# Copying a row to all partitions: products with constant matrices replaced by DMAs through DRAM, in a two-layer decoder trunk

## The chip, the cores and the metric

The kernel runs on one core of a Trainium2 chip. The metric is the device time of one execution in microseconds. A core has five engines that run their own instruction streams in order: TensorE (PE, matrix products into PSUM; its weight loads are listed as PEld), VectorE (DVE), ScalarE (ACT), GpSimd (POOL) and SyncE (SP), which here only issues DMAs. Streams wait for each other by semaphores, and for DMAs in the same way. DMAs are issued from SP, ACT or POOL and carried by 16 DMA engines.

## What is computed

Two layers over 512 tokens of width 1024. Each layer normalises x, multiplies it with one wide matrix, runs sliding-window attention and an mLSTM on slices of the result, merges both under gates, and adds a squared-ReLU MLP. Cut to what the change touches:

```python
def rmsnorm(x, gain):
    x32 = x.astype(jnp.float32)
    inv = lax.rsqrt(jnp.mean(x32 * x32, axis=-1, keepdims=True) + EPS)   # one factor per token
    return (x32 * inv).astype(x.dtype) * gain

h = rmsnorm(x, norm_mix)
z = h @ w_in
q_a, k_a, v_a, q_m, k_m, v_m, o_m, if_m, gates = jnp.split(z, splits, axis=-1)
...
# mLSTM, per head and chunk: a running maximum over the tokens keeps the exponentials bounded
log_d = jnp.where(causal, b[..., :, None] - b[..., None, :] + log_i[..., None, :], -jnp.inf)
m_t = jnp.maximum(log_inter, jnp.max(log_d, axis=-1))
w = jnp.exp(log_d - m_t[..., None]) * jnp.einsum('bnhlk,bnhsk->bnhls', q, k)
...
g_a, g_m = jnp.split(gates, 2, axis=-1)
mixed = jax.nn.sigmoid(g_a) * (att @ w_att_branch) + jax.nn.sigmoid(g_m) * (hm @ w_m_branch)
x = x + mixed @ w_out
x = x + relu(rmsnorm(x) @ W1)^2 @ W2
```

## The kernel before

Tokens go in four blocks of 128 (`NB`), features in eight (`KT`). Every weight matrix is streamed from DRAM in chunks of 128 x 512 (SP issues the loads), and each chunk is split into a high part `wh` (ACT, L165) and a low part `wl` (DVE, L166), both in a reduced-precision float32 form; the activations are split in the same way. One block of a product is then three matmuls (`mm3`): high x high, high x low, low x high. A chunk feeds four blocks, which go to four PSUM banks; a group is eight chunks (four for the branch projections), and after it ACT or DVE empties the four banks (`evac`). There are five banks for these products and three, `aux`, for everything else. The split tiles have four buffers.

The mixer of a layer (`mixer`) runs the groups in this order: q, then k, v and the gate logits (264 columns), then the mLSTM's q and k (`ev_qk`), two groups of branch gates, the mLSTM's v (`ev_v`, banks emptied by ACT at L711), the two halves of the attention projection, and more. Into these, `weave` puts the side work at given places: attention by units of a block and a kv head (`att_scores`, `att_softmax`, `att_probs`, `att_out`), the mLSTM's gating (`gating0` to `gating3`), and for each of its four heads `m_decay`, `m_weights` and `m_out`. A scheduler then settles the order of each engine's stream from the dependencies, priorities and its own costs; the order on ACT, DVE and POOL follows from that.

Two places copy a row to all 128 partitions.

**The norm's factor.** It exists as a column, one value per token and partition (`norm.col`, 128 x 4, last written at L244). q and k/v of the attention, and v of the mLSTM, have tokens on the partitions and use the column. The mLSTM's q and k and the branch gates have tokens along the free dimension and need the factor as a row of 512 in every partition. `along` makes it: four DVE multiplies build diagonal matrices from the identity (L297), a product with a matrix of ones sums them in PSUM, and ACT copies the result to SBUF (L302). The row is read by DVE in `ev_qk` (L665, L667) and for the gates (L699). Behind it on POOL come the squares of q (L505), whose sums DVE takes (L506).

**The running maxima.** `gating2` makes `cm`, four rows (one per head) of 512 running maxima, by scans on DVE (L474). `gating3` splits them into a high part on partitions 0 to 3 and a low part on partitions 32 to 35 of `cm2` (L492, L493). `m_decay` multiplies `cm2` with a selector `sel`, prepared by POOL for each layer, so that one head's row appears in all partitions of an `aux` bank, and ACT copies it to a temporary (L741). `m_weights` reads it: DVE takes a maximum (L748), ACT exponentials (L749, L752), POOL masks the triangle (L754), and DVE multiplies with a product of keys and queries (L760).

Of the kernel before, what the change touches and what calls it, by code (L numbers as in the profile page):

```python
# [8 lines left out]
F32 = mybir.dt.float32  # L9
F32R = mybir.dt.float32r  # L10
BF16 = mybir.dt.bfloat16
I32 = mybir.dt.int32
AF = mybir.ActivationFunctionType
ALU = mybir.AluOpType
AX = mybir.AxisListType

P = 128
T = 512
NB = T // P
# [6 lines left out]
MH, MQK, MV = 4, 64, 128  # L26
# [7 lines left out]
def hybrid_kernel(ctx, tc, x, norm_mix, w_in, att_q_norm, att_k_norm, att_sinks, m_gate_bias,  # L34
# [3 lines left out]
    ve, sc, gp = nc.vector, nc.scalar, nc.gpsimd  # L38

    latest = [None]  # L40
# [15 lines left out]
    small = ctx.enter_context(tc.tile_pool(name="small", bufs=3))  # L56

    inp = ctx.enter_context(tc.tile_pool(name="inp", bufs=2))

    uid = [0]  # L60

    def nm(s):
        uid[0] += 1
        return f"{s}_{uid[0]}"
# [4 lines left out]
    def pool(phase, name, bufs):  # L69
        now[name] = phase.enter_context(tc.tile_pool(name=name, bufs=bufs, reuse_waits="tile"))  # L70
        return now[name]
# [4 lines left out]
    def temp(dt=F32):  # L76
        return now["tmp"].tile([P, T], dt, tag="t", name=nm("t"))
# [14 lines left out]
    def aux(shape=(P, T)):  # L92
        return now["paux"].tile(list(shape), F32, tag="aux", name=nm("aux"))
# [4 lines left out]
    def f32(ap):  # L98
        return ap.bitcast(F32)


    start = ExitStack()
    psum_pools(start, 3)
    sc.preload_act_table_set(LN_EXP)
    ident = const.tile([P, P], F32, name="ident")
    make_identity(nc, ident)
    ones = const.tile([P, P], F32, name="ones")
# [5 lines left out]
                     pattern=[[1, P]], channel_multiplier=-1)  # L113
    gp.affine_select(out=tri_l, in_=ones, compare_op=ALU.is_ge, fill=0.0, base=0,
                     pattern=[[-1, P]], channel_multiplier=1)
# [130 lines left out]
    class Norm:  # L246
# [45 lines left out]
        def along(self):  # L292

            with tc.high_priority():
                dg = temp()
                for b in range(NB):
                    ve.tensor_scalar(dg[:, b * P:(b + 1) * P], ident, self.col[:, b:b + 1], None, op0=ALU.mult)  # L297
                pb = aux()
                with tc.issue_after(latest[0].ins):
                    pe.matmul(pb, ones, dg, start=True, stop=True)  # L300
                row = temp()
                sc.activation(row, pb, AF.Copy)  # L302
            return row


# [82 lines left out]
    def mixer(l, norm, late, order, phase):  # L388
# [6 lines left out]
        mid = pool(phase, "mid", 1)  # L395
# [8 lines left out]
        row = []  # L404
# [73 lines left out]
                                     gr[:, b:b + 1], op=ALU.add)  # L478


        sel = mid.tile([P, MH, P], F32R, tag="sel", name=nm("sel"))
        gp.memset(f32(sel), 0.0)
        for r in (0, 32):
            gp.affine_select(out=sel[r:r + MH], in_=ones[r:r + MH, 0:1].unsqueeze(2).to_broadcast([MH, MH, P]),
                             compare_op=ALU.is_equal, fill=0.0, base=0,
                             pattern=[[-1, MH], [0, P]], channel_multiplier=1)
        cm2 = mid.tile([P, T], F32R, tag="cm2", name=nm("cm2"))
        gp.memset(f32(cm2), 0.0)

        def gating3():  # L490
            cm = cms[0]
            sc.activation(cm2[0:MH, :], cm, AF.Copy)  # L492
            ve.tensor_tensor(cm2[32:32 + MH, :], cm, f32(cm2[0:MH, :]), op=ALU.subtract)  # L493
            cps = aux([P, NB * MH])
            for b in range(NB):
                pe.transpose(cps[:, b * MH:(b + 1) * MH], cm[:, b * P:(b + 1) * P], ident[:MH, :MH])
            ve.tensor_tensor(em.rearrange("p b h -> p (b h)"), cps,
                             bl[:, 0].rearrange("p b h -> p (b h)"), op=ALU.add)
            sc.activation(em, em, AF.Exp, scale=-1.0)
# [3 lines left out]
        for b in range(NB):  # L503
# [5 lines left out]
                         op=ALU.mult)  # L509
# [207 lines left out]
        for i, (b, kv) in enumerate(units):  # L717
# [6 lines left out]
            if kv == 0 and b + 1 < NB:  # L724
                if b + 2 < NB:
                    side += [(at + 1, lambda b=b: k_vec(b + 2)), (at + 1, lambda b=b: q_vec(b + 2))]
                side += [(at + 2 * 1.65 - 1.75, lambda b=b: k_tr(b + 1)), (at + 2 * 1.65 - 2.15, lambda b=b: q_tr(b + 1))]
        side += [(8.45 + 3.0 * i, f) for i, f in enumerate((gating0, gating1, gating2, gating3))]
        side += [(9.6 + 1.65 * n, lambda n=n: qk_split(n // 2, n % 2)) for n in range(8)]
        g0, s0 = gate_steps(0)  # L730
# [4 lines left out]
        cmbs, wts = {}, {}  # L735

        def m_decay(h):
            pb = aux()
            pe.matmul(pb, sel[:, h, :], cm2, start=True, stop=True)
            cmbs[h] = temp()  # L740
            sc.activation(cmbs[h], pb, AF.Copy)  # L741

        def m_weights(h, s):
            cmb = cmbs[h]
# [56 lines left out]
        for h in range(MH):  # L801
            at = 28 + 4.65 * h
            side.append((at, lambda h=h: m_decay(h)))
            for i in range(NB):
                side += [(at + 1.75 + 4.65 * i / NB, lambda h=h, i=i: m_weights(h, i)),
                         (at + 4.65 + -0.55 + 4.65 * (i + 0.5) / NB, lambda h=h, i=i: m_out(h, i))]
# [513 lines left out]
    for l in range(DEPTH):  # L1320
        with start if l == 0 else ExitStack() as phase:
            if l > 0:
                psum_pools(phase, 3)
            norm = mixer(l, norm, late, order, phase)
        late = norm.steps(1, 1.5, 0.5)
        with ExitStack() as phase:
            psum_pools(phase, 2)
            norm = mlp(l, norm, late, phase)
        late = norm.steps(0, 1.5, 0.5, lambda k, norm=norm: turn_behind(norm, k)) if norm else []
        order = [4, 5, 6, 7, 0, 1, 2, 3]  # L1330
# [40 lines left out]
```

## Time and profile before

| | us |
|---|---|
| median of 3 runs | 1303.78 |
| lowest and highest run | 1303.59, 1304.21 |
| span of the profiled execution | 1302.9 |
| ACT busy | 763.7 |
| DVE busy | 955.5 |
| POOL busy | 200.4 |
| first and last copy of the norm's row to SBUF (L302) starts at | 39.8, 684.4 |
| first and last copy of a head's maxima to SBUF (L741) starts at | 152.3, 844.1 |

The span runs from the first to the last instruction of one profiled execution; the time of a run lies a little above it, as it has what comes before and after. In the rows of the trace a line of the timeline gives the start in us, the duration in us, the engine, the source line, the operation, the tile that it writes and those that it reads, the shape, how many equal instructions are merged (x), and in brackets how long the engine had been idle and what released it. Matmul durations overlap, since matmuls are pipelined; the distance between their starts is what one costs. A row of the waits gives the waiting engine and operation, what it waited for, the total in us, the number of waits and the longest. A row of DMA issues gives what is loaded, the issuing queue, the count, the size and the median time in us from issue to landing.

### The profile page before, as it was taken

The numbers are of one execution on the slowest core, as the hardware profiler recorded it, in microseconds if no ns is written. First come the engines' busy times: TensorE is split into PE (matmuls) and PEld (weight loads), VectorE is DVE, ScalarE is ACT, GpSimd is POOL, SyncE is SP. The second block draws the span as 40 slices with busy tenths as digits, with TensorE's granted clock in tenths as the row PEclk, the third lists the DMA queues.
The fourth block names the chain that finished last, engine by engine and source line by source line (L and its number), as shares of the span: only waits on it lengthen the run. The fifth ranks groups of instructions, "written<-read, shape, count | busy, mean of one in ns | idle before, by whom it ended". The sixth has DMA issues, their size and how long they took to land. (4 is left out here: it accounts for less than half of the span.)

```text
span 1302.9 us, 19074 instructions
## 1 busy us (share of the span) xinstructions
PE 1291.5 (99%) x6978; PEld 1105.2 (85%) x6978; DVE 955.5 (73%) x1505; ACT 763.7 (59%) x1329; POOL 200.4 (15%) x281
## 2 busy tenths in 40 slices
PE   9999999999999999999999999999999999999998
PEld 6877788888889999999888778888888899999987
DVE  4699754475677897968948996545737878879797
ACT  5578755544466665656555787554445556665563
POOL 4511100000003021131115111000000030311210
PEclk9999999999999999999999999999999999999999
DMA  5422222372369888898124222223714597988953
GB/s 154 110 72 59 74 81 74 90 249 82 98 155 172 236 185 207 195 211 216 33 75 114 65 66 75 79 75 92 256 57 129 141 215 195 201 212 196 213 148 98
DMA packets 130542, 177.61 MB, mean 136 GB/s; under 512 B 9864, under 2 KB 78320, under 8 KB 130448
## 3 DMA queue, kind: packets, MB, share of 16 engines
q1 hardware_dynamic: 94208, 131.82, 32.7%
q0 software_dynamic: 35520, 44.17, 21.2%
q8 instruction: 55, 0.90, 0.3%
q10 hardware_dynamic: 720, 0.40, 0.1%
q14 instruction: 39, 0.32, 0.1%
HBM read 174.27 MB, written 2.10 MB: 135 GB/s over the span
## 5 line engine op out<-in xcount | busy, mean ns | idle before, releaser
L47 PE MATMUL mm<-i,wh 128*128 128x512 f32 (+1 forms) x1280 | 352.7, 362 | 0.0
L867 ACT ACTIVATE wh<-raw 128x1024 fp32r<-128x1024 f32 x212 | 223.1, 1056 | 181.1 <-PE mm L47 114.0
L868 DVE TENSOR_TENSOR wl<-raw,wh 128x1024 fp32r<-128x1024 f32 x212 | 255.2, 1218 | 74.2 <-ACT wh L867 72.3
L47 PEld LDWEIGHTS mm<-i,wh 128*128 128x128 f32 x1280 | 224.3, 189 | 32.1 <-DVE a L699 0.8
L166 DVE TENSOR_TENSOR wl<-w,wh 128x512 fp32r<-128x512 f32 (+1 forms) x208 | 140.8, 679 | 137.7 <-ACT wh L165 129.4
L47 PE MATMUL mm<-i,wl 128*128 128x512 f32 (+1 forms) x640 | 229.8, 360 | 0.0
L165 ACT ACTIVATE wh<-w 128x512 fp32r<-128x512 f32 (+1 forms) x208 | 127.0, 611 | 146.7 <-PE mm L47 122.8
L47 PE MATMUL mm<-wh,uh 128*128 128x512 f32 x440 | 171.8, 390 | 0.0
L47 PE MATMUL mm<-wl,uh 128*128 128x512 f32 x440 | 171.7, 390 | 0.0
L47 PE MATMUL mm<-wh,ul 128*128 128x512 f32 x440 | 171.2, 389 | 0.0
L1027 POOL DMA_DIRECT2D raw<-in_w_ff_dram x48 | 62.3, 1304 | 591.3 <-DMA raw<-in_w_ff_dram 316.9
L47 PE MATMUL mm<-wh,i 128*128 128x512 f32 (+1 forms) x512 | 150.6, 370 | 1.2 <-ACT wh L165 0.6
L47 PEld LDWEIGHTS mm<-i,wl 128*128 128x128 f32 x640 | 120.8, 189 | 18.1 <-DVE wl L868 0.4
L47 PEld LDWEIGHTS mm<-wh,i 128*128 128x128 f32 x512 | 92.0, 188 | 19.0 <-DVE i L179 2.1
L913 DVE SCALAR_TENSOR_TENSOR x<-mm,ms,x 128x512 f32<-128x512 f32 x126 | 90.4, 743 | 9.9 <-PE mm L47 9.9
L47 PEld LDWEIGHTS mm<-wh,ul 128*128 128x128 f32 x440 | 82.6, 188 | 17.4
L47 PEld LDWEIGHTS mm<-wh,uh 128*128 128x128 f32 x440 | 82.8, 188 | 16.1
L47 PEld LDWEIGHTS mm<-wl,uh 128*128 128x128 f32 x440 | 82.8, 188 | 15.6
L47 PE MATMUL mm<-wl,i 128*128 128x512 f32 (+1 forms) x256 | 93.0, 363 | 0.0
L47 PE MATMUL mm<-wh,a 128*128 128x512 f32 x256 | 81.3, 392 | 0.0
L47 PE MATMUL mm<-a,wh 128*128 128x512 f32 x256 | 80.5, 397 | 0.0
L47 PE MATMUL aux<-i,wh 128*128 128x256 f32 x384 | 69.5, 283 | 0.0
(259 smaller groups left out, 2161.0 us busy)
## 6 DMA issues: line engine op xcount, KB each, us to landing
raw<-in_w_ff_dram SPq DMA_DIRECT2D x144, 512.0 KB, 5.2
raw<-in_w_ff_dram POOLq DMA_DIRECT2D x84, 512.0 KB, 7.8
w<-in_w_in_dram SPq DMA_DIRECT2D x128, 256.0 KB, 2.6
w<-in_w_out_dram SPq DMA_DIRECT2D x32, 256.0 KB, 2.7
w<-in_w_att_branch_dram SPq DMA_DIRECT2D x16, 256.0 KB, 2.6
w<-in_w_m_branch_dram SPq DMA_DIRECT2D x16, 256.0 KB, 2.7
w<-in_w_in_dram SPq DMA_DIRECT2D x16, 128.0 KB, 2.1
out_dram<-x SPq DMA_DIRECT2D x7, 256.0 KB, 2.0
```

The source lines that it names most:

```text
L47: latest[0] = nc.tensor.matmul(*args, **kw)
L165: sc.activation(wh[:, :off], raw[:, :off], AF.Copy)
L166: ve.tensor_tensor(wl[:, :off], raw[:, :off], f32(wh[:, :off]), op=ALU.subtract)
L867: sc.activation(hi, src, AF.Copy)
L868: ve.tensor_tensor(lo, src, f32(hi), op=ALU.subtract)
L913: ve.scalar_tensor_tensor(xh[:, cc], ps[i][:, cc], ms[j][:, b:b + 1], xh[:, cc], op0=ALU.mult, op1=ALU.add)
L1027: gp.dma_start(to[h], src(h, i, j), accum_op=ALU.add)
```

## The change

Both copies go through DRAM. A pool of DRAM tiles, `rows`, is added. `along` writes the column to a DRAM line of 512 floats, token order, and reads that line back into all partitions of a temporary; both DMAs are issued from POOL. `gating3` writes the four rows of `cm` to a DRAM tile `decay`, and `m_decay` reads one head's row into all partitions of a temporary, again from POOL. The diagonal multiplies, the products with `ones` and `sel`, the copies from PSUM, `sel`, `cm2` and the split of `cm` fall away. What reads the rows is unchanged.

```diff
     inp = ctx.enter_context(tc.tile_pool(name="inp", bufs=2))
+    rows = ctx.enter_context(tc.tile_pool(name="rows", bufs=2, space=bass.MemoryType.DRAM))
...
         def along(self):
 
             with tc.high_priority():
-                dg = temp()
-                for b in range(NB):
-                    ve.tensor_scalar(dg[:, b * P:(b + 1) * P], ident, self.col[:, b:b + 1], None, op0=ALU.mult)
-                pb = aux()
-                with tc.issue_after(latest[0].ins):
-                    pe.matmul(pb, ones, dg, start=True, stop=True)
+                line = rows.tile([T], F32, tag="line", name=nm("line"))
+                gp.dma_start(line.rearrange("(b p) -> p b", p=P), self.col)
                 row = temp()
-                sc.activation(row, pb, AF.Copy)
+                gp.dma_start(row, line.partition_broadcast(P))
             return row
...
-        sel = mid.tile([P, MH, P], F32R, tag="sel", name=nm("sel"))
-        gp.memset(f32(sel), 0.0)
-        for r in (0, 32):
-            gp.affine_select(out=sel[r:r + MH], in_=ones[r:r + MH, 0:1].unsqueeze(2).to_broadcast([MH, MH, P]),
-                             compare_op=ALU.is_equal, fill=0.0, base=0,
-                             pattern=[[-1, MH], [0, P]], channel_multiplier=1)
-        cm2 = mid.tile([P, T], F32R, tag="cm2", name=nm("cm2"))
-        gp.memset(f32(cm2), 0.0)
+        decay = rows.tile([MH, T], F32, tag="decay", name=nm("decay"))
 
         def gating3():
             cm = cms[0]
-            sc.activation(cm2[0:MH, :], cm, AF.Copy)
-            ve.tensor_tensor(cm2[32:32 + MH, :], cm, f32(cm2[0:MH, :]), op=ALU.subtract)
+            gp.dma_start(decay, cm)
...
         def m_decay(h):
-            pb = aux()
-            pe.matmul(pb, sel[:, h, :], cm2, start=True, stop=True)
             cmbs[h] = temp()
-            sc.activation(cmbs[h], pb, AF.Copy)
+            gp.dma_start(cmbs[h], decay[h].partition_broadcast(P))
```

In the order of the changed streams, the four broadcasts of a layer stand on POOL behind the last attention mask (heads 0 and 1), behind the first mask of head 1 (head 2) and behind the first mask of head 2 (head 3); the exponentials and maxima of heads 1 to 3 stand earlier on ACT and DVE than before, ahead of or among the evictions of the mLSTM's v. The reductions of L506 stand among the weight splits of the k/v group, the first behind that of its fourth chunk. On PE, apart from the removed products, a few transposes and products of the attention stand some matmuls earlier.

## Prediction

> **What bounds the kernel now.** I read first the page's head, busy times and slices, then TensorE's waits.
>
> ```profile
> span 1302.9 us, 19074 instructions
> PE 1291.5 (99%) x6978; PEld 1105.2 (85%) x6978; DVE 955.5 (73%) x1505; ACT 763.7 (59%) x1329; POOL 200.4 (15%) x281
> PE   9999999999999999999999999999999999999998
> PEclk9999999999999999999999999999999999999999
> ```
> ```profile
> PE aux L47 <- ACT t L581: 2.0, 2, 1.3
> PE aux L47 <- POOL ones L108: 1.2, 1, 1.2
> PE aux L52 <- ACT wh L165: 1.1, 2, 0.6
> ```
>
> PE is busy for 99% of the span, in every slice and at the full granted clock; its three largest waits are 2.0, 1.2 and 1.1 us. So a matmul taken from PE's stream shortens the span by its own time, and a new wait lengthens it only where PE itself stops. ACT, DVE and POOL may wait as long as PE's next operand is ready.
>
> **What is removed from PE.** Per layer one fp32 product with `ones` and four with `sel`. Busy times overlap with neighbours, so the price is read from the starts around them; the last row has the count of the `sel` products.
>
> ```profile
> 38.60 0.28 PE L47 MATMUL mm<-wh,i 128*128 128x264 f32 x1
> 38.73 1.02 PE L47 MATMUL aux<-t,ones 128*128 128x512 f32 x2
> ...
> 39.83 0.40 PE L47 MATMUL mm<-wh,i 128*128 128x264 f32 x2
> ...
> 40.19 0.40 PE L47 MATMUL mm<-wh,i 128*128 128x264 f32 x2
> ```
> ```profile
> 151.03 0.40 PE L47 MATMUL aux<-cm,sel 128*128 128x512 f32 x1
> 151.27 0.40 PE L47 MATMUL mm<-wh,i 128*128 128x512 f32 x1
> ```
> ```profile
> L47 PE MATMUL aux<-cm,sel 128*128 128x512 f32 x8 | 3.2, 394 | 0.0
> ```
>
> A usual block of three matmuls lasts 40.19 - 39.83 = 0.36 us; the block with the `ones` product lasts 39.83 - 38.60 = 1.23. The product costs 0.87 us, twice 1.74. A `sel` product costs 151.27 - 151.03 = 0.24, eight cost 1.9. **PE loses 3.6 us.** The four L297 multiplies, both evictions (L302, L741), the split of `cm` (L492, L493) and POOL's fills and selects for `sel` and `cm2` go too; none released PE, so they count nothing.
>
> **What a copy through DRAM takes.** The trace has no such copy. The nearest rows:
>
> ```profile
> w<-in_w_att_branch_dram SPq DMA_DIRECT2D x16, 256.0 KB, 2.6
> w<-in_w_in_dram SPq DMA_DIRECT2D x16, 4.0 KB, 1.9
> gc<-in_att_q_norm_dram POOLq DMA_DIRECT2D x2, 0.4 KB, 2.5
> grow<-in_m_head_norm_dram POOLq DMA_DIRECT2D x1, 4.0 KB, 2.2
> grow<-in_norm_ffn_dram POOLq DMA_DIRECT2D x1, 8.0 KB, 3.8
> gbias<-in_m_gate_bias_dram POOLq DMA_DIRECT2D x1, 8.0 KB, 4.2
> cosx<-in_rope_cos_dram POOLq DMA_DIRECT2D x1, 32.0 KB, 6.6
> ```
>
> A broadcast writes 128 rows of 2 KB, 256 KB, like a weight chunk. From SP the size costs 2.6 - 1.9 = 0.7 us; a small quiet POOL issue lands after 2.2. I take L = 2.2 + 0.7 = 2.9 us from issue to landing. The low end is 2.2, as if size cost nothing; the high end is 6.6, the slowest POOL row, which ran beside the first loads of x. That 128 readers share one row seems cheap: `gbias`, read that way, took 4.2 against 3.8 for `grow`, unshared, in the same crowd; 4.2 + 0.7 = 4.9 is the middle case.
>
> A weighing of its own: the profile's row for POOL's issues in the busy MLP is
>
> ```profile
> L1027 POOL DMA_DIRECT2D raw<-in_w_ff_dram x48: 1280/1286/1469, 346.8 to 1218.7; - x48
> ```
>
> so no issue was held more than 0.18 us over the median. The Trainium skill ("SBUF — State Buffer", section "SBUF: two separate sides") speaks against the change: descriptors for a POOL-issued DMA cannot be written while VectorE holds the shared port, and such a DMA of some 620 ns took 3100 there. By that rule L grows by about 2.5 us (an estimate from the page) to the second rival's case; by the row it stays, and the row decides here.
>
> **The norm's factor (`along`).** POOL issues a write of 512 single elements to DRAM, waits until it has landed, then issues the broadcast. Both stand in POOL's queue ahead of the squares of q (L505), and POOL waits for them.
>
> ```profile
> 31.85 0.16 DVE L244 TENSOR_TENSOR ncol<-ncol,nru 128x4 f32<-128x4 f32 x1
> 33.41 4.43 POOL L505 TENSOR_TENSOR t<-a 128x512 f32<-128x512 f32 x4 [9.36 <-ACT a L407]
> 39.73 1.86 DVE L506 TENSOR_REDUCE ssq<-t 128x8 f32<-128x512 f32 x3
> 39.38 0.43 DVE L166 TENSOR_TENSOR wl<-w,wh 128x264 fp32r<-128x264 f32 x1 [1.00 <-ACT wh L165]
> 68.41 1.27 DVE L665 SCALAR_TENSOR_TENSOR a<-mm,t 128x512 f32<-128x512 f32 x2
> 671.15 0.16 DVE L244 TENSOR_TENSOR ncol<-ncol,nru 128x4 f32<-128x4 f32 x1
> 678.04 4.43 POOL L505 TENSOR_TENSOR t<-a 128x512 f32<-128x512 f32 x4 [29.14 <-ACT a L407]
> 8.48 0.94 POOL L353 DMA_DIRECT2D cosx<-in_rope_cos_dram  x1
> 12.13 0.55 POOL L361 DMA_DIRECT2D gbias<-in_m_gate_bias_dram  x1
> ```
>
> The factor is ready at 32.0. The single elements cost about 0.4 us more to issue than `gc` (0.94 for `cosx`' 512 pieces against 0.55 for 128), so the write lands near 32.0 + 2.5 + 0.4 = 34.9, and POOL is free at 35.5 after 0.55 for the second issue. The row itself is there near 38; its first reader, L665, starts at 68.4, so that latency is hidden 30 us deep.
>
> The danger is POOL's delay. In the changed order of layer 0 DVE's reductions L506 stand ahead of some weight splits: before the split for the sixth k/v chunk DVE has done three. A square lasts 1.11 us, a reduction and a split end 0.67 + 0.43 after the third, so that split ends 4.4 us after POOL is free. PE wants it at the sixth chunk: the fourth started at 38.7 (the `ones` product stands at its head), a chunk is four blocks, 1.44 us, and without the product the sixth starts at 41.6. POOL must be free by some 37.3. With 35.5 nothing stops; with `cosx`' 6.6 POOL is free at 39.2 and PE stops 1.9. In layer 1 the squares start 6.7 us after the factor (678.0 against 671.3), so even that end costs next to nothing. Term: 0, bounds 0 to 1.9.
>
> **The running maxima.** `decay` (8 KB) is written once the last scan (L474) is done, at 113.2 us, 6.7 us before POOL's next select at 119.9. The four broadcasts stand in POOL's queue: heads 0 and 1 behind the last attention mask, head 2 behind head 1's first mask, head 3 behind head 2's first. Since no product of PE orders them any longer, the exponentials of all four heads move forward on ACT, and ACT must finish them before it empties PE's banks of v.
>
> ```profile
> 112.68 0.47 DVE L474 TENSOR_TENSOR_SCAN t<-aux,mp,neg 4x128 f32<-4x128 f32 x1
> 119.89 0.64 POOL L634 TENSOR_SCALAR_AFFINE_SELECT t<-t 128x512 fp32r<-128x512 f32 x1 [13.43 <-DVE kT L561]
> 147.91 2.11 POOL L634 TENSOR_SCALAR_AFFINE_SELECT t<-t 128x512 fp32r<-128x512 f32 x3 [0.23 <-DVE t L176]
> 154.76 0.39 ACT L749 ACTIVATE t<-t,bias 128x128 f32<-128x128 f32 x1
> 155.06 0.39 ACT L752 ACTIVATE t<-t,bias 128x128 f32<-128x128 f32 x1
> 161.16 2.05 ACT L711 ACTIVATE vm<-mm,ncol 128x512 f32<-128x512 f32 x3 [0.41 <-PE mm L47]
> 163.92 0.63 PE L47 MATMUL mm<-a,wh 128*128 128x512 f32 x2
> 806.41 2.05 ACT L711 ACTIVATE vm<-mm,ncol 128x512 f32<-128x512 f32 x3 [0.41 <-PE mm L47]
> ```
>
> On the old clock: the selects end at 150.0, so head 0 lands at 150.0 + L. Eleven exponentials at 0.30 and a weight split (0.53) follow until head 1's first mask may run: 3.8, the mask 0.3, then head 2's copy: it lands at 154.1 + 2L. Behind it on ACT stand one exponential (0.3, with DVE's maximum 0.25 ahead of it) and the first L711 (0.6). PE needs that bank for the second block of the next product, 163.92 less one removed `sel` product, 163.7. So head 2 must land by 162.5, that is **L up to 4.2 us is free**. With 2.9 it lands at 159.9, 2.6 us early. Layer 1 repeats this 645.25 us later (806.41 against 161.16). DVE's maxima wait at the same place, ahead of weight splits that PE wants about two chunks (5 us) later. Head 3 lands near 165.5, where DVE handles the first output. Term: 0; at L = 4.9 2 x (163.9 - 162.5) = 2.8.
>
> **Moved order.** The transposes of attention's seventh unit move up by eight matmuls (1.8 us) on PE, and the product behind them now needs a bank that ACT and DVE empty after a table load; I count a stop of up to 0.9 us per layer. In exchange a subtraction of the k split leaves DVE's path to the transposes before, where the old wait of 0.6 per layer (1.1 in the quoted row) should go. Taken as 0; bounds -1.1 and +1.8.
>
> **Sum.** 1302.9 - 3.6 = 1299.3 us of span. The runs' median, 1303.78, is 0.9 above this span, so the time is **1300.2 us**, 0.27% less. Its own range with the moved order is 1299.1 to 1302.0.
>
> **Rivals.**
>
> Late broadcasts: L = 4.9. For it: the shared row and POOL's issue path are untried here; against: at 150 us the DMA engines are far less loaded than at 12 us, where `gbias` ran. 1300.2 + 2.8 = 1303.0. Chance 0.18.
>
> Slower: the broadcasts take 6.6 us or more, and head 2's copy, needed by an exponential in front of L711, stops PE in both layers: 2 x (154.1 + 13.2 - 162.5) = 9.6, with 1.9 for the norm 1311.7. It decides from about L = 5.8, where the stops, 2 x 3.2, exceed gain and measuring bound together. For it: the copy is chained twice, so each microsecond counts double; against: the only rows above 5 us that are as small ran beside the loads of x. Chance 0.15.
>
> A late write of the single elements, 6.6 us, and nothing else: 1302.1. The Trainium skill ("DMA: Bandwidth & Descriptors", sections "Specifications" and "Rules for kernel authors") holds that a non-contiguous last dimension becomes one descriptor per element and that pieces under 512 B are read, modified and written; no run here shows that for a store, and the page gives no time for it, so the rows' bounds stand. Chance 0.06.
>
> No gain: PE stops for ACT or DVE as long as the removed products lasted. The small waits speak against it. 1303.8. Chance 0.07.
>
> **How the numbers follow.** My forecast has the remaining 0.54. The runs can tell 0.2%, 2.6 us, from no change. Faster: 0.54 for the forecast. Slower: 0.15. The other rivals fall within the bound: 0.31. The range leaves out the slower rival and a little below: 1299.1 to 1305.0.
>
> **What would show it.** Right: no `sel` or `ones` products of 128x512 on PE after the start, broadcasts that land under 4.2 us, POOL's squares starting by 37 us in layer 0, no new PE wait above 1 us, v's evictions unmoved. Wrong: a PE wait released by ACT L711's counterpart or by DVE's `wl` in the k/v chunks, with ACT or DVE idle until a DMA of `decay` or `line`.

## The result, and the profile after

| | before | changed |
|---|---|---|
| time, median (us) | 1303.72 (1303.59 to 1304.21) | 1314.16 (1313.69 to 1314.77) |
| span of the profiled execution (us) | 1302.9 | 1311.8 |
| mean granted clock in it | 1.000 | 0.995 |
| all PE waits in it, summed (us) | 6.6 | 12.8 |

The changed kernel is slower: ratio 1.008, interval 1.0067 to 1.0092. The forecast of 1300.2 us with its range to 1305.0 was wrong.

The page's head, the 40 slices and PE's longest waits, of the changed kernel:

```profile
span 1311.8 us, 19048 instructions
...
PE 1293.4 (99%) x6966; PEld 1106.9 (84%) x6966; DVE 953.6 (73%) x1495; ACT 757.6 (58%) x1317; POOL 203.1 (15%) x287
...
PE   9899999999999999999999999999999999999998
...
PEclk9899999999999999999999999999999999999999
```
```profile
PE mm L47 <- DVE wl L167: 8.4, 2, 5.7
PE aux L47 <- POOL ones L109: 1.2, 1, 1.2
PE aux L47 <- ACT t L570: 1.1, 2, 0.6
```

PE executes 12 matmul instructions fewer (an fp32 product counts as two), and the old wait of `aux` for ACT's `wh` is gone. One new wait outweighs that: two stops, together 8.4 us, for DVE's low parts `wl`, and the slice that holds the first of them is the only one with a lower clock. The DMA issues of the changed kernel say where to look:

```profile
t<-decay POOLq DMA_DIRECT2D x8, 256.0 KB, 3.7
...
t<-line POOLq DMA_DIRECT2D x2, 256.0 KB, 4.7
...
line<-ncol POOLq DMA_DIRECT2D x2, 2.0 KB, 8.9
...
decay<-t POOLq DMA_DIRECT2D x2, 8.0 KB, 2.5
```

The broadcasts are near what was forecast. The write of 2 KB as 512 single elements takes 8.9 us, more than twice the 3.7 us of a broadcast of the maxima, which carries 256 KB. The timeline of layer 0 around it, from POOL, DVE, ACT and PE in turn:

```profile
31.80 0.83 POOL L297 DMA_DIRECT2D line<-ncol  x1 [9.47 <-DVE ncol L245]
40.73 0.56 POOL L299 DMA_DIRECT2D t<-line  x1 [8.09 <-DMA line<-ncol]
41.30 4.02 POOL L494 TENSOR_TENSOR t<-a 128x512 f32<-128x512 f32 x4
```
```profile
42.39 0.69 DVE L495 TENSOR_REDUCE ssq<-t 128x8 f32<-128x512 f32 x1 [7.39 <-POOL t L494]
42.99 2.63 DVE L167 TENSOR_TENSOR wl<-w,wh 128x264 fp32r<-128x264 f32 x1
```
```profile
35.54 0.42 ACT L166 ACTIVATE wh<-w 128x264 fp32r<-128x264 f32 x1 [0.44 <-PE mm L47]
40.72 0.42 ACT L166 ACTIVATE wh<-w 128x264 fp32r<-128x264 f32 x1 [4.75 <-DMA w<-in_w_in_dram]
```
```profile
45.68 0.59 PE L47 MATMUL mm<-wl,i 128*128 128x264 f32 x1 [5.74 <-DVE wl L167]
```

Read from the end: PE stops 5.74 us for a `wl`. That split should take 0.43 us and took 2.63; it ended at 45.62, 0.30 after POOL's last square (41.30 + 4.02 = 45.32). Before it DVE sat 7.39 us in front of a reduction, because POOL had waited 8.09 for the write. The `wh` that this split needs had been ready since 35.54 + 0.42 = 35.96, so POOL's lateness and not late weights made this stop. But ACT's next `wh` had no weights until 40.72, just when the write landed. So there are two suspects: POOL's lateness, and late weights that the stop may hide. The DMA issues of the window from 33 to 36 us, of the changed kernel and then of the kernel before, show the second one plainly:

```profile
w<-in_w_in_dram SPq DMA_DIRECT2D x1, 128.0 KB, 7.4
w<-in_w_in_dram SPq DMA_DIRECT2D x2, 4.0 KB, 7.7
```
```profile
w<-in_w_in_dram SPq DMA_DIRECT2D x2, 128.0 KB, 2.0
w<-in_w_in_dram SPq DMA_DIRECT2D x1, 4.0 KB, 1.9
```

Weight loads that SP issues in this window, while POOL's write is under way, land after 7.4 us (128 KB) and 7.7 us (4 KB, median of two) in place of 2.0 and 1.9.

### The profile page after: what moved, and what is told of

It is laid out like the page before. It is cut to its first block, busy times and chain, and to the rows that moved or that the text cites. A ratio compares the mean times of both kernels' runs of the same rounds, so it can differ in the third digit from the quotient of the medians.

```text
span 1311.8 us, 19048 instructions
## 1 busy us (share of the span) xinstructions
PE 1293.4 (99%) x6966; PEld 1106.9 (84%) x6966; DVE 953.6 (73%) x1495; ACT 757.6 (58%) x1317; POOL 203.1 (15%) x287
## 5 line engine op out<-in xcount | busy, mean ns | idle before, releaser
L167 DVE TENSOR_TENSOR wl<-w,wh 128x512 fp32r<-128x512 f32 (+1 forms) x208 | 143.9, 695 | 128.2 <-ACT wh L166 122.9
L47 PEld LDWEIGHTS mm<-wh,i 128*128 128x128 f32 x512 | 94.7, 194 | 17.1 <-DVE i L180 1.5
```

Of the source, the lines that this page charges most:

```text
L47: latest[0] = nc.tensor.matmul(*args, **kw)
L167: ve.tensor_tensor(wl[:, :off], raw[:, :off], f32(wh[:, :off]), op=ALU.subtract)
```

## The experiments

Theory 1: POOL is held by the write, so its squares are late, and with them what DVE has behind its reductions. Theory 2: the write holds up the weight loads. A rival puts the loss on the broadcasts of `decay` and the attention order that moved with them.

| run | what it is | us | ratio to before, interval |
|---|---|---|---|
| e1_decay_only | maxima through DRAM, factor by product | 1303.32 | 0.9997, 0.9988 to 1.0006 |
| e2_line_only | factor through DRAM, maxima by product | 1316.71 | 1.0103, 1.0089 to 1.0117 |
| e3_read_late | changed, row read behind the squares | 1310.20 | 1.0045, 1.0032 to 1.0058 |
| e4_pieces16 | changed, write in 128 pieces | 1311.85 | 1.0059, 1.0047 to 1.0072 |
| e5_fix | 128 pieces, read late, no stride in evictions | 1303.17 | 0.9997, 0.9987 to 1.0006 |
| e6_reduce_late | changed, reductions behind the splits | 1317.80 | 1.0107, 1.0092 to 1.0122 |
| e7_fill | changed, products in PE's stops | 1316.62 | 1.0098, 1.0083 to 1.0113 |
| e8_dead_write | before, plus an unread write, 512 pieces | 1312.80 | 1.0070, 1.0053 to 1.0087 |
| e9_rows512 | changed, write as 4 rows of 512 bytes | 1301.60 | 0.9985, 0.9976 to 0.9994 |
| e10_dead_256 | before, plus an unread write, 256 pieces | 1303.75 | 1.0001, 0.9992 to 1.0011 |
| e11_dead_128 | before, plus an unread write, 128 pieces | 1303.83 | 1.0001, 0.9992 to 1.0010 |
| e12_hold_only | e9, squares held back without a slow DMA | 1305.20 | 1.0010, 1.0001 to 1.0020 |

### Which half of the change

e1 takes `along` back to the product (its diff below), e2 takes `m_decay` and `gating3` back.

```diff
-                line = rows.tile([T], F32, tag="line", name=nm("line"))
-                gp.dma_start(line.rearrange("(b p) -> p b", p=P), self.col)
+                dg = temp()
+                for b in range(NB):
+                    ve.tensor_scalar(dg[:, b * P:(b + 1) * P], ident, self.col[:, b:b + 1], None, op0=ALU.mult)
...
+                    pe.matmul(pb, ones, dg, start=True, stop=True)
```

> Only the running maxima go through DRAM; the norm's factor is again a product with ones. Theory 1 (POOL is held while it waits for the line write of 512 single elements, so the squares and with them DVE's weight splits are late) and theory 2 (the weight loads that are issued while that write is under way land late) both expect the time before less eight sel products of 0.24 us: 1303.7 - 1.9 = 1301.8 us, no PE wait above 1.2 us. Rival (the four broadcasts of a layer, or the order of the attention that moved with them, cost the time): 1308 us or more.

> Only the norm's factor goes through DRAM; the maxima are again products with sel. Theories 1 and 2: the changed kernel's time plus the eight sel products, 1314.2 + 1.9 = 1316.1 us, with the two PE stops of about 5.7 and 2.6 us behind DVE's wl in the k/v chunks. Rival (broadcasts or moved order): near 1303.7 - 1.7 = 1302.0 us.

The whole loss comes with the norm's factor: e2 has it (1316.7), e1 has not (1303.3), and e1's longest PE wait is the old one, 1.2 us at the start. The rival falls. But e1 misses its 1301.8: against before, the maxima's part gains 0.3 us, not 1.9. Between e2 and the changed kernel the same part is worth 2.5 us (1316.71 against 1314.16); the section on the prediction comes back to this.

### POOL's wait, or the loads

e3 moves only the read, behind the square of k (`sqk_`); POOL does its squares while the write runs.

```diff
-                row = temp()
-                gp.dma_start(row, line.partition_broadcast(P))
...
+        with tc.issue_after(sqk_.ins):
+            gp.dma_start(row[0], line.partition_broadcast(P))
```

> The changed kernel, with the read of line placed in POOL's queue behind the squares of q and k instead of ahead of them. The write is the same 512 single elements, but POOL waits for it only when its squares are done. Theory 1: the PE stops in the k/v chunks vanish, the clock stays at 1.00, 1300.2 us. Theory 2: the write still delays the weight loads issued beside it (landing 7 us and more, against 1.9 to 2.1), PE still stops some 1 to 2 us in each layer, 1302 to 1305 us.

1310.2: above even the second theory's 1302 to 1305. Its POOL, ACT and PE rows of layer 0:

```profile
32.37 4.23 POOL L492 TENSOR_TENSOR t<-a 128x512 f32<-128x512 f32 x4 [0.20 <-ACT a L402]
```
```profile
42.74 0.42 ACT L166 ACTIVATE wh<-w 128x264 fp32r<-128x264 f32 x1 [7.25 <-DMA w<-in_w_in_dram]
```
```profile
43.22 0.39 PE L47 MATMUL mm<-wh,i 128*128 128x264 f32 x1 [2.43 <-ACT wh L166]
```

The squares are on time, and PE stops all the same, now for ACT's `wh`, before which ACT sat 7.25 us without weights. e8 asks the same from the other side: the kernel before, with the write added in `along` and nobody reading it.

```diff
+                line = rows.tile([T], F32, tag="line", name=nm("line"))
+                gp.dma_start(line.rearrange("(b p) -> p b", p=P), self.col)
                 dg = temp()
```

> The kernel before, with the write of line (512 single elements from ncol, same place in POOL's queue) added; nothing reads it and nothing waits for it. Its direct cost is 0.8 us of POOL per layer. Theory 1 (POOL's wait): within 1 us of before, 1303.7 to 1304.7 us. Theory 2 (the write holds up the weight loads issued beside it): loads landing at 6 us and more, PE stops for ACT wh in the k/v chunks, and as much more as the run with the late read stands above the forecast, 1310.2 - 1300.2 = 10 us: about 1313 us.

A write that no instruction waits for costs 8.9 us (1312.8 against 1303.9). Layer 0 of e8, ACT and then PE:

```profile
42.95 0.42 ACT L166 ACTIVATE wh<-w 128x264 fp32r<-128x264 f32 x1 [7.02 <-DMA w<-in_w_in_dram]
45.75 0.42 ACT L166 ACTIVATE wh<-w 128x264 fp32r<-128x264 f32 x1 [2.38 <-DMA w<-in_w_in_dram]
```
```profile
43.42 0.39 PE L47 MATMUL mm<-wh,i 128*128 128x264 f32 x1 [1.34 <-ACT wh L166]
...
52.70 0.73 PE L47 MATMUL mm<-i,wh 128*128 128x512 f32 x2 [1.59 <-ACT kvi L413]
```

So late loads alone can cost most of what the change lost. The Trainium skill ("DMA: Bandwidth & Descriptors", section "Queues, rings and completion order") says that each DMA engine takes the queues in turn but drains a whole packet of one before it goes to the next; a packet of many slow single elements would hold SP's loads in that way. The late loads here agree with that (7.4 against 2.0 us); no run here shows the order inside an engine.

### What of the order on DVE

e6 keeps the slow write and POOL's wait, and puts DVE's reductions behind the last split of the k/v chunks (`last_wl`).

```diff
-            ve.tensor_reduce(ssq[:, b, 0:8], sq.rearrange("p (h d) -> p h d", d=HD), axis=AX.X, op=ALU.add)
+            with tc.issue_after(last_wl[0].ins):
+                ve.tensor_reduce(ssq[:, b, 0:8], sq.rearrange("p (h d) -> p h d", d=HD), axis=AX.X, op=ALU.add)
...
```

> The changed kernel, with DVE's reductions of the squares behind all weight splits of the k/v chunks. POOL is held as before and its squares start near 41.3 us. Theory 1 (the reductions ahead of the splits carry POOL's delay to PE): 1300.2 us. Theory 2 (late weight loads alone): PE stops for ACT wh as in the run with the late read, 1310 us. If POOL's run of four squares also holds DVE's two-operand splits (the split of 2.63 us that ended 0.3 us after the last square): such a split again, ending 0.3 us after the squares, and 1312 to 1314 us.

1317.8, worse than the changed kernel and above all three answers expected; its write took longer too, 11.0 us in layer 0. Theory 1 in its simple form, the reductions as carriers, falls. POOL and DVE of layer 0:

```profile
43.81 4.03 POOL L495 TENSOR_TENSOR t<-a 128x512 f32<-128x512 f32 x4
```
```profile
43.67 5.14 DVE L168 TENSOR_TENSOR wl<-w,wh 128x264 fp32r<-128x264 f32 x3 [7.13 <-ACT wh L167]
```
```profile
43.67 4.45 DVE L168 TENSOR_TENSOR wl<-w,wh 128x264 fp32r<-128x264 f32 x1 [7.13 <-ACT wh L167]
```

Three splits that take 0.4 us each lasted 5.14 together, with no reduction between them. Taken singly (the last row, from a narrower window), the first lasted 4.45 us and ended at 48.12, 0.28 after POOL's last square (43.81 + 4.03 = 47.84); the other two followed in 0.7. So squares back to back hold the split itself. e12 tests that with no slow DMA in the kernel: e9 (below), with POOL's squares behind a 1x1 copy from a late weight tile.

```diff
+        held_ = gp.tensor_copy(held, f32(whs[(-2, -5)[l]][0:1, 0:1]))
...
+            with tc.issue_after(held_.ins):
                 sq_ = gp.tensor_tensor(sq, q_tok[b], q_tok[b], op=ALU.mult)
```

> The run with rows of 512 bytes (1301.6 us), with POOL's squares held back by data instead of by a DMA: a 1x1 copy on POOL reads the seventh k/v chunk's high part in layer 0 (ready near 41 us, where the changed kernel's squares began) and the fourth's in layer 1 (near 688 us). No slow DMA is in this kernel, so the weight loads land in time; DVE's reductions stand behind eight (layer 0) and four (layer 1) of the weight splits. If four squares back to back hold DVE's two-operand splits until they end (4.0 us, as the splits of 2.63 and 5.14 us in the other runs suggest), a split of the last k/v chunks ends 0.3 us after the last square, near 45.5 us, PE stops 1.5 to 3 us in each layer, and the time is 1304.6 to 1308 us. If squares and splits run beside each other: no PE stop above 0.5 us there and 1301.6 to 1302 us; POOL's lateness alone is then nothing.

1305.2, 3.6 us over e9: the time is inside the expected 1304.6 to 1308, the stops are not what was expected. POOL and DVE of layer 0, then the same split of DVE in layer 1:

```profile
39.71 4.03 POOL L500 TENSOR_TENSOR t<-a 128x512 f32<-128x512 f32 x4
```
```profile
42.38 1.65 DVE L169 TENSOR_TENSOR wl<-w,wh 128x264 fp32r<-128x264 f32 x1
...
683.62 1.65 DVE L169 TENSOR_TENSOR wl<-w,wh 128x264 fp32r<-128x264 f32 x1
```

The split ended at 42.38 + 1.65 = 44.03, again 0.29 after the last square (43.74). PE did not stop for it. It stopped behind the k/v chunks, for ACT's eviction of them, 1.18 us in layer 0 (ACT had sat 3.06 us without weights just before) and 0.25 in layer 1, where 1.5 to 3 in each were expected; and in the attention it waited 2.6 us for ACT's `t` (L583), 1.1 in e9. So the hold of the split is shown, and that late squares cost 3.6 us; how they cost it in the attention was not followed. The Trainium skill ("SBUF — State Buffer", section "SBUF: two separate sides") says that VectorE with two SBUF inputs and GpSimd share a port under a lock that is held for a whole instruction. The trace agrees that the split is blocked (2.63 us in place of 0.43), and goes beyond it: in the changed kernel the split began in the second square and outlasted the third and fourth too. In the kernel before a split that fell among the squares took only 0.67 us; what decides whether it slips in between two squares was not found.

### How many pieces

e4 lets each partition write its four factors as one piece of 16 bytes; the row then holds the tokens in another order, and the evictions view it with a stride.

```diff
-                gp.dma_start(line.rearrange("(b p) -> p b", p=P), self.col)
+                gp.dma_start(line.rearrange("(p b) -> p b", b=NB), self.col)
...
-            return row
+            return row.rearrange("p (q b) -> p b q", b=NB)
...
```

> The changed kernel, with line laid out so that each partition writes its four factors as one piece of 16 bytes: 128 pieces in place of 512, the same 2 KB; the row is read as one 2 KB row as before, and the DVE evictions of q, k and the gates view it with a stride. Order of all engines as in the changed kernel. If the number of pieces sets the write's time (8.9 us for 512, so near 2.5 to 4 us for 128), POOL is free in time and the weight loads are not delayed: no PE stop above 1.2 us, 1300 to 1301 us by theory 1 and theory 2 alike. If the write's time comes from being a write to DRAM with a read behind it, whatever its pieces: landing still 8 to 9 us, 1314 us.

The write's part came as expected, the time did not. The trace's issue of the write, its evictions of the gates and its largest PE wait:

```profile
line<-ncol POOLq DMA_DIRECT2D x2, 2.0 KB, 2.1
```
```profile
L689 DVE TENSOR_TENSOR a<-mm,t 128x512 f32<-128x512 f32 x32 | 32.4, 1062 | 0.0
```
```profile
PE aux L47 <- ACT t L570: 4.6, 2, 3.0
```

2.1 us for the same 2 KB, and no stop above 0.6 us in the k/v chunks. But an eviction that reads the row with a stride takes 1062 ns, against 682 in the changed kernel, and PE now waits 4.6 us in the attention, in two waits. The loss has moved: from the first eviction of k/v to the first of the mLSTM's v, where q, k and half of the gates are evicted, the layers take 121.6 and 119.3 us, against 116.0 and 115.9 in the changed kernel. That the stride causes this is likely, and no run changes the stride alone. e5 keeps the 128 pieces, reads late, and puts the row in order once per layer on ACT.

```diff
...
+        side.append((5.5, lambda: sc.activation(row[0].rearrange("p (b q) -> p q b", b=NB),
+                                                mixed_row.rearrange("p (q b) -> p q b", b=NB), AF.Copy)))
```

> Both cures together: the write in 128 pieces of 16 bytes, and the read of the row behind the squares in POOL's queue; the row is put in its order once per layer by ACT (1 instruction of some 0.7 us, about 7 us before the first eviction that reads it), so the DVE evictions read it without a stride (680 ns against 1062 in the run with 128 pieces alone). If pieces, POOL's wait and the strided evictions are the whole loss: no PE stop above 1.2 us, loads beside the write landing within 4 us, clock 1.00, 1300.2 to 1302 us. If something else of the change costs the time: 1305 us or more.

1303.2: 11 us of the loss are back, but it stands 1.2 us above the expected range; its added ACT copy (1.12 us, not 0.7) stands among the evictions of the attention's transposed q, and for these (L573) PE waits 3.6 us. The trace is of an execution of 1305.1 us, 2 us above the median, so the median's share of this wait is not known. e10 and e11 are e8 with 256 and 128 pieces.

> The kernel before with an unread write of ncol in 256 pieces of 8 bytes (the 512 single elements, unread, added 8.9 us). If the harm grows with the number of pieces above some 128 that do none: landing 4 to 6 us, and a third of 8.9, 3 us more: 1306.7 us. If any write from ncol with pieces under 16 bytes does the full harm: 1312 us.

> The kernel before with an unread write of ncol in 128 pieces of 16 bytes. By the run with both cures (landing 1.9 us, loads beside it 1.9 to 3.0): no harm, 1303.7 us. If 128 pieces harm in proportion, a quarter of 8.9: 1305.9 us.

Both cost nothing that can be told (1303.75 and 1303.83 against 1303.62, intervals of about 1.2 us either way), so the harm to the time is not in proportion. The view of the write in e11, e10 and e8 lists landings, shortest, median and longest; for e8 the trace has the landing of layer 1 only:

```profile
DMA to landing us min/median/max: 1.8/2.7/3.6
```
```profile
DMA to landing us min/median/max: 4.3/4.9/5.5
```
```profile
DMA to landing us min/median/max: 12.1/12.1/12.1
```

The loads beside the write took up to 4.4 us with 128 pieces, up to 5.7 with 256, and up to 11.9 in e8 with 512. With 256 PE did not stop in the k/v chunks: the chunks loaded ahead cover that much, and not what 512 pieces bring. In all these runs the 2 KB stay the same, so the number of pieces and their size change together; which of the two counts is not shown.

### The clock

In the changed kernel PE's granted clock falls behind both stops (windows of core 0; after the engines' busy times come clock, DMA share and GB/s):

```profile
40.00:46.00 6.00, 0.32 (x1) 0.32 (x2) 3.61 (x3) 0.84 (x2) 4.58 (x5) 0.81 0.49 47
46.00:50.00 4.00, 4.00 (x19) 4.00 (x19) 2.52 (x6) 0.43 (x1) 0.00 (x0) 0.50 0.53 125
...
692.00:696.00 4.00, 3.33 (x16) 3.33 (x17) 2.92 (x6) 0.42 (x1) 0.32 (x1) 0.57 0.29 68
```

e7 fills the stops with products that nobody reads.

```diff
+            for _ in range((6, 3)[l]):
+                with tc.high_priority(), tc.issue_after(latest[0].ins):
+                    pe.matmul(pf, ones, ones.unsqueeze(1).to_broadcast([P, NB, P]), start=True, stop=True)
...
```

> The changed kernel, with fp32 products of ones with ones (128x512, 0.87 us each) put into PE's stream where it stops: six ahead of the fifth k/v chunk of layer 0 (5.2 us in a stop of 5.7) and three ahead of the fourth of layer 1 (2.6 in a stop of 2.6). Their result is not read. If PE's stop is what makes the granted clock fall (0.50 over 46 to 50 us, 0.57 over 692 to 696 us): the clock stays at 1.00 and the time falls by what the slow clock cost, 4 x 0.50 + 5 x 0.05 + 3.3 x 0.43 = 3.7 us, to 1310.5 us, though PE does more work. If the clock falls for another reason (the DMA traffic, a fixed time): 1314 us and the same low clock.

The clock stays at 1.00 in all these windows, so the stop is what lowers it. The time does not fall; it rises by 2.4 us. In this run the write took 9.7 us, and with the clock up PE ran into the next late load: ACT's `wh` at 51.07 had waited 6.81 us for its weights. So a faster clock had little to work on; what the low clock costs by itself was not separated, and the 3.7 us of the expectation stay an estimate from the windows.

### A version that beats both

e9 turns the factor's column into four rows on PE (one 128x4 transpose per layer, at a somewhat earlier place in the weave), writes those rows behind the squares of q (`sq_`), and reads them behind the square of k (`sqk_`).

```diff
+                turned = aux([NB, P])
+                with tc.issue_after(latest[0].ins):
+                    pe.transpose(turned, self.col, ident)
+                four = sm([NB, P], "four", 2)
+                sc.activation(four, turned, AF.Copy)
...
+        with tc.high_priority(), tc.issue_after(sq_.ins):
+            gp.dma_start(line, four)
...
+        with tc.issue_after(sqk_.ins):
+            gp.dma_start(row[0], line.rearrange("b p -> (b p)").partition_broadcast(P))
```

> The changed kernel with the factor's column turned into four rows by one 128x4 transpose on PE (0.1 us per layer) and one small ACT eviction, written to DRAM as 4 pieces of 512 bytes behind the squares in POOL's queue, and read behind the squares of k. No stride in any eviction, no single elements. If single elements and POOL's place are the whole loss, the forecast for the change holds but for the transposes: 1300.2 + 0.2 = 1300.4 us, loads in the k/v chunks landing at 1.9 to 3 us, PE waits as in the run with only the maxima through DRAM. If the kernel stays at 1302.5 to 1303.7, as the run with both cures did, the 3.6 us taken from PE do not reach the end of the span even without the write's harm.

1301.6 us, 0.9985 of before (0.9976 to 0.9994): faster than both, 1.2 us short of the expected 1300.4. Its write, and the weight loads beside it between 33 and 44 us:

```profile
w<-in_w_in_dram SPq DMA_DIRECT2D x2, 128.0 KB, 2.1
w<-in_w_in_dram SPq DMA_DIRECT2D x2, 4.0 KB, 1.9
line<-four POOLq DMA_DIRECT2D x1, 2.0 KB, 1.7
```

The same 2 KB in four pieces lands after 1.7 us and no load is late. Pieces, their source and POOL's order changed together here, so their shares are not told apart.

## Why the prediction was wrong, step by step

**The step that failed** is the line write in the norm's factor: "so the write lands near 32.0 + 2.5 + 0.4 = 34.9". It priced 512 single elements as a load of 0.4 KB and a longer issue, and took the slowest POOL row, `cosx` with 6.6, as the worst case; but that row's 512 pieces had 64 bytes each and were read from DRAM. Written as 4 bytes each they took 8.6 and 9.1 us. From this came the term "0, bounds 0 to 1.9", which should have been some 12.6: so much the changed kernel stands above e9.

**What it never asked** is what the write does to other transfers. It followed POOL's queue and the row's latency, and took SP's loads as given. An unread write alone costs 8.9 (e8).

**Where the loss lies** can be read from stages. From the column's last write to the first product of the mLSTM's q and k the changed kernel takes 22.2 and 23.6 us in the two layers, before 14.8 and 20.1: 10.8 us more. The two stops (8.4) and the slow clock behind them (3.7, the estimate of e7), less the two products with `ones` (1.7), make 10.4 of it. Late squares alone (e12 against e9) leave this stage at 14.2 and 19.5 us; they lengthen the next one, to the first product of the attention projection, from 116.4 and 116.3 us to 118.6 and 117.8, and in the changed kernel this one takes 116.4 and 116.3 too. So the prices of single causes do not add up to the changed kernel's loss: that 8.9 (e8), 3.6 (e12 against e9) and -2.0 (e9 against before) sum to 10.5, near its 10.4, is chance. In the changed kernel the two causes overlap: the late weights were hidden behind the stop that POOL made, and come out when POOL's wait is taken away (e3, 1310.2).

**PE's deadline** was nearly right in kind. The prediction had POOL needed by 37.3 for the sixth k/v chunk behind three reductions; PE stopped one chunk earlier, behind one reduction, and the split was not only queued but blocked for 2.2 us more.

**Layer 1** "costs next to nothing", since the squares started 6.7 us after the factor there. With a write of 9.1 us they were 3.9 us late (688.29 against 677.7 + 6.7 = 684.4), and PE stopped 2.63.

**The maxima.** L was taken as 2.9 with up to 4.2 free; the broadcasts landed in 3.4 to 4.7, median 3.7, and no PE wait above 0.6 us stands between 60 and 265 us. DVE waited 7.9 us for them, in four waits, and that cost PE nothing, as forecast. Head 2's copy, which decided in the prediction, landed after 3.7 and 3.6. Of the two answers weighed for POOL's issues, the row's held: the issues of these copies took 537 to 583 ns in the changed kernel, and no growth like that of the Trainium skill's example ("SBUF — State Buffer", section "SBUF: two separate sides") appears (the copies landed 0.8 later than L). By the Trainium skill's example L would have been 2.9 + 2.5 = 5.4, which is short of the 6.6 of the second rival, not its case. The rivals of late broadcasts fell; that the slower one said 1311.7, near the measured time, is chance, since its cause did not occur. v's evictions moved later by 1.4 us against the start of this stage (116.35 us after the first eviction of k/v in e1, 114.97 before) without a stop.

**PE's gain** of 3.6 reached the time in part: e9, which lacks some 0.2 of it for its transposes, stands 2.0 below before. The product with `ones` fits its price of 1.74: e9 gains 1.7 over e1, though each of the two times is known to about 1.2 us only. The eight `sel` products, priced at 0.24 each from two starts, gave 0.3 with an interval of -1.6 to +0.8 us between e1 and before, so 1.9 is just outside; between e2 and the changed kernel they gave 2.5. The traces show six of them near their price: three of a layer's four stand between the first `mm<-a,wh` and the last `mm<-wh,a` of the layer, and this stage takes 170.80 and 170.74 us before, 170.16 and 170.15 in e1, so about 0.2 for each product. The first head's stands in the stage before it, from the first product of the mLSTM's q and k, and there the traces show no clear gain (116.23 and 116.84 us before, 116.57 and 116.43 in e1), though the wait of `aux` for `wh` left it too. Why that stage did not shrink is open.

**The moved order** brought no new wait: the old wait of `aux` for `wh` vanished, and that for ACT's `t` fell from 2.0 to 1.1 us. Whether it cost something without a listed wait is open, as is the stage just named. The rival of a late write alone (1302.1, chance 0.06) had the right place and a sixth of the size.

## What to carry to other kernels

Price a small DMA by its pieces and their size, not by its bytes: turning the column into rows on PE before it goes to DRAM, and keeping the write behind POOL's work, were together worth 12.6 us here (1314.2 against 1301.6). Ask of every new DMA not only who waits for it but which transfers are issued while it runs; a write that nobody read cost 8.9 us. And an operation on POOL that is late can block DVE, even where DVE's queue does not stand behind it (the split of 4.45 us in e6). Prices that single-cause runs give need not add up where the causes overlap: look at which stage each of them lengthens.

## What was not expected of the hardware

512 single elements of 4 bytes took 8.6 to 12.1 us to DRAM, 256 of 8 bytes 4.3 to 5.5, 128 of 16 bytes 1.8 to 3.6, four of 512 bytes 1.6 to 1.7. Loads of another queue, issued while the 512 elements were written, took up to 8.5 us in the changed kernel and up to 11.9 in e8, in place of 1.9 to 2.1. DVE's two-operand split of 0.43 us lasted until 0.3 us after the last of POOL's back-to-back squares, up to 4.45 us (e6). After PE's stops of 5.7 and 2.6 us the granted clock was 0.50 and 0.57 for about 4 us; after one of 2.1 us in e5 it was 0.53 for the next 2 us. A DVE eviction that reads one operand at a stride of 16 bytes took 1062 ns instead of 682.
